# Dealing transposes out between short value products, and summing squares by transposes and row sums, in a hybrid decoder layer

## The chip, the cores and the metric

The kernel runs on one core of a Trainium2 chip. The metric is the device time of one execution in microseconds (us); lower is better. Three runs of the kernel before the change took 1103.09, 1104.46 and 1104.14 us. The chip's engines are named as in the profile: PE (TensorE matmuls), PEld (the weight loads of TensorE, which run beside its matmuls), DVE (VectorE), ACT (ScalarE), POOL (GpSimd) and SP (SyncE, which here issues the transfers).

## What is computed

One decoder layer on 1024 tokens of width 1024 in fp32, cut to what matters:

```python
h = rms_norm(x, ln_pre_mix)
proj = h @ w_in
q, k = rope(q, pos), rope(k, pos)
pool_out = multi_scale_pool(u_pool, w_pool, pool_scale)
attn_out = dilated_attention(q, k, v)
mix = concatenate([pool_out, attn_out]) @ w_out
x = x + rms_norm(mix, ln_post_mix)
h = rms_norm(x, ln_pre_ffn)
f = (silu(h @ w_gate) * (h @ w_up)) @ w_down
x = x + rms_norm(f, ln_post_ffn)

def rms_norm(x, g):
    return x * rsqrt(mean(x * x, axis=-1) + EPS) * g
```

The attention has 12 heads of dimension 64. Each head is evaluated under three (window, dilation) settings, (128, 1), (512, 4) and (2048, 16), and the three results are merged by their softmax denominators.

## The kernel before

**Numbers.** Activations lie with the channels on the 128 partitions and the tokens along the row. Every large product is made of fp32 numbers split in a high and a low part: hi is a copy rounded to the fast fp32 format, lo is the rest. A product is three matmuls (hi by hi, hi by lo, lo by hi), which is why most rows of the profile come in threes. A split is an ACT copy (hi) and a subtraction on DVE or POOL (lo): L340 and L344 for one family of weights, L1484 and L1486 for the gate and up weights, L1780 to L1782 for the down weights.

**Stages.** Norm and input projections; then attention; then the output projection, norm and residual (about 410 to 480 us), the SwiGLU block with its three large products (to about 1090), and the last norm with the residual. The 1024 tokens are worked in two halves of 512, and the heads in six pairs, so attention has 12 units (pair, half). Between the steps of a unit stand projection products as filling.

**Order.** The plan of the attention is a table of places (`put`, with a number per step) written by hand. All matmuls and transposes keep the order in which the program makes them: `mm` and `turned_to` both end in `keep_in_program_order`. DVE, ACT, POOL and SP take their order from a scheduler with priorities. PE reads its queue strictly in order.

**Values of a unit.** `values` makes the steps that turn probabilities into outputs. A step `turn` transposes three or four 128 x 128 tiles of the weighed probabilities `pp` on PE into a bank of PSUM (tag "t", of which there are two), by the matrix `pmt` or the identity `idt`; ACT then copies the bank to the hi part of `ptr` (L969) and DVE forms its lo part (L970). There are two buffers `ptr`. A step `product` multiplies the columns of `ptr` by the values `v`: per tile (or per two to four neighbouring tiles, if they share their keys) a pair of matmuls, one on the hi columns with 128 columns of weights, one on the lo columns with 64. Half 0 has three groups a head (4, 3 and 3 tiles), half 1 four groups of 4, of which two have four pairs of 128 columns each.

In six of the units (1, 3, 5, 7, 8 and 11, marked `tv`) turns and products are joined: the step `both(i)` makes the products of two groups, then the turns of the next two. In units 1, 3, 5, 7 and 11 that gives runs of 16 short products followed by 8 transposes. The other six units have turns and products as separate steps, each at its own place in the plan.

**Norms.** The sum of squares over the channels of a token crosses the partitions. For four of the norms (two halves of the norm after the mixer, two of the one ahead of the SwiGLU block) `Squares.add` collects the squares of eight blocks of channels in `sq` (ACT squares into `p`, DVE adds), and `Squares.mean` multiplies each 128 tokens of `sq` by a column of ones, which leaves 128 sums in the rows of a bank: four matmuls of one column, each in two passes, so eight records in the trace. `rsqrt_mean` takes them through ACT (L365, and L369 for a second use of the sum) and a power of -0.5 on POOL (L370). `Squares.rows` then spreads the result along the partitions with four transposes of `nrr`, and the norm's scaling on DVE reads them.

The last norm is in `End`. Its `mean` for half 0 multiplies both `sq` and the last block's squares `p`, which were not added yet, by the ones: twice four matmuls. Its first step behind the sums is on DVE (L367), then the power on POOL (L370).

Of the kernel before, what the change touches and what calls it, by code (L numbers as in the profile page):

```python
# [8 lines left out]
F32 = mybir.dt.float32  # L9
# [18 lines left out]
EARLY = 6  # L28

# [261 lines left out]
def hybrid_block(ctx: ExitStack, tc: tile.TileContext, xT, w_in, w_v, w_vp, w_pool, w_out, w_gate, w_up, w_down,  # L291
# [80 lines left out]


# [13 lines left out]
    ones = const.tile([P, 217], F32, name="ones")[:, :1]  # L387
# [556 lines left out]
    def values(pr, h):  # L944
# [7 lines left out]

        def turn(hd, gi):
            g = groups[gi]
            if h:
                need(("w", pr.p, h, hd, g[0][0]), 4)
            else:
                need(("w", pr.p, 0, hd), 4)
            await_(("t", 0), weighted(hd, gi))
            t = bank("t")  # L960
            for n, (kb, j) in enumerate(g if h == 0 else ()):
                turned_to(t[:, n * P:(n + 1) * P], un.row(hd, j)[:, kb * P:(kb + 1) * P], pmt)
            for n, (side, kb, qs, part) in enumerate(g if h else ()):
                turned_to(t[:, n * P:(n + 1) * P], un.pp[hd, side][:, qs, part * P:part * P + P],
                                    idt if side else pmt)
            w = len(g) * P
            ptr = turned[hd, gi] = att.tile([P, 2, 512], F32R, name="ptr", tag="ptr", bufs=PTB)
            with tc.high_priority(offset=rank("t", pr, h)):
                nc.scalar.activation(ptr[:, 0, :w], t[:, :w], AF.Copy)  # L969
                nc.vector.tensor_tensor(ptr[:, 1, :w], t[:, :w], ptr[:, 0, :w].bitcast(F32), ALU.subtract)  # L970
            turned_in(("ptr", pr.p, h, hd, gi))

        def product(hd, gi):
# [11 lines left out]
            if h == 0:  # L985
                for kb in sorted({kb for kb, j in g}):
# [5 lines left out]
                    mm(oo[0:64], v[:, 0], ptr[:, 1, n * P:n * P + wd], start=False, stop=(kb == 3), skip_group_check=True)  # L992
                    n += 4 - kb
            while h and n < len(g):
# [5 lines left out]
                else:  # L1000
# [7 lines left out]
                   start=False, stop=last, skip_group_check=True)  # L1008
                n += wd // P
# [15 lines left out]
        def both(i):  # L1025
            old, new = ids[max(0, 2 * i - 2):2 * i], ids[2 * i:2 * i + 2]
            if i:
                await_(*([("t", 0), ("t", 1)] if new else []),
                       *(weighted(*a) for a in new),
                       *(("ptr", pr.p, h, *a) for a in old), ("v", pr.p, h))  # L1030
            for a in old:
                product(*a)
            for a in new:
                turn(*a)
        return ([lambda a=a: turn(*a) for a in ids], [lambda a=a: product(*a) for a in ids],
# [162 lines left out]
    for u, (pr, h) in enumerate(units):  # L1198
# [12 lines left out]
        def part(n, i, a=(pr, h), box=box):  # L1211
# [849 lines left out]
```

## Time and profile before

| | us |
|---|---|
| runs of the kernel, three | 1103.09, 1104.46, 1104.14 (median 1104.14) |
| the profiled execution: span from the first to the last instruction | 1101.3 |
| what lies around the span, against the median | 2.8 |
| DMA, mean over the span | 183 GB/s |
| POOL, the power L370 of the norms, 128x4, five times | 1.10 each |
| DVE, row sum L871 (128x128 to 128x32), six times | 0.28 each |

The profiled execution's own time is its span and what lies around it; differences worked out in the span carry over to the time as they are.

How to read the rows. A row of the timeline is: start in us from the span's start, length in us, engine, line of the kernel, operation, result <- operands, for a matmul the size of the array used, shapes, how many such instructions in a row, and in brackets how long the engine idled ahead of it and what ended that. A run's length goes from its first start to its last end; the instructions in it overlap, since PE is pipelined. A row of groups has the count, then the busy time and the mean ns of one, then the idle time ahead of them with what ended it.

### The profile page before, as it was taken

Reading aid. Unit: us, or ns where it says so; the run is one execution under the profiler, and the core shown is the slowest. Engines: PE = TensorE matmul, PEld = TensorE weight load, DVE = VectorE, ACT = ScalarE, POOL = GpSimd, SP = SyncE. Lnnn points to the kernel's source line nnn. Section 1 sums busy time; section 2 is a strip of 40 time slices with the busy share of each in tenths; the row PEclk is TensorE's granted clock in tenths of the full one; section 3 lists DMA queues with packets and bytes.
Section 4 is the critical chain, followed back from the end, with each engine's and each line's share of the span. In section 5 each row is a group of like instructions: output and inputs, shape, how many; then the busy total and the mean of one; then the engine's idle time right before and its main releaser. Section 6 shows DMA issues by size and latency. Waiting matters only on the chain.

```text
span 1101.3 us, 16033 instructions
## 1 busy us (share of the span) xinstructions
PE 1091.4 (99%) x5653; PEld 930.7 (85%) x5653; DVE 796.7 (72%) x1350; ACT 553.8 (50%) x994; POOL 519.9 (47%) x421
## 2 busy tenths in 40 slices
PE   9999999999999999999999999999999999999998
PEld 7888999998898888888888888888888888888887
DVE  7967878777977758799677778576566576343674
ACT  7456767676777855765322222233222534343432
POOL 0001616263654120100677777677568958666521
PEclk9999999999999999999999999999999999999999
DMA  8225232424248448554466766443455878656442
GB/s 297 96 83 182 97 135 78 153 94 156 77 173 325 173 147 302 222 199 168 179 235 240 239 241 227 172 172 134 143 200 199 291 265 281 207 182 201 134 153 77
DMA packets 91296, 201.81 MB, mean 183 GB/s; under 512 B 9296, under 2 KB 25168, under 8 KB 89808
## 3 DMA queue, kind: packets, MB, share of 16 engines
q1 hardware_dynamic: 90240, 200.00, 51.8%
q8 instruction: 44, 0.72, 0.3%
q10 hardware_dynamic: 976, 0.79, 0.2%
q14 instruction: 36, 0.29, 0.1%
HBM read 143.87 MB, written 56.89 MB: 182 GB/s over the span
## 4 chain that ended last, share of the span: by engine, by line
PE 97%; ACT 1%; DVE 1%; DMA 0%; issue 0%; POOL 0%; ACTq 0%; DVEq 0%
PE ps_pj L296 31%; PE ps_s L296 26%; PE ps_o L296 26%; PE ps_t L296 10%; PE ps_t L299 3%; DMA wraw<-in_w_in_dram 0%; ACT pp L834 0%; PE ps_o L299 0%; ACT ptr L969 0%; ACT z L1302 0%; POOL rcl L538 0%; POOL rsw L535 0%; ACT whl L340 0%; DVE y L1899 0%; ACT k L557 0%
## 5 line engine op out<-in xcount | busy, mean ns | idle before, releaser
L296 PE MATMUL ps_o<-tT,fw 128*128 128x512 f32 x648 | 150.4, 389 | 0.0
L296 PEld LDWEIGHTS ps_o<-tT,fw 128*128 128x128 f32 x648 | 121.6, 188 | 25.2
L296 PE MATMUL ps_pj<-x,whl 128*128 128x512 f32 x480 | 130.6, 398 | 0.0
L1486 POOL TENSOR_TENSOR fw<-rw,fw 128x512 fp32r<-128x512 f32 x72 | 99.9, 1410 | 34.1 <-ACT fw L1484 34.1
L296 PEld LDWEIGHTS ps_pj<-x,whl 128*128 128x128 f32 x480 | 86.5, 188 | 14.0
L344 POOL TENSOR_TENSOR whl<-wraw,whl 128x512 fp32r<-128x512 f32 x42 | 57.4, 1389 | 49.7 <-ACT whl L340 41.0
L1781 POOL TENSOR_TENSOR op<-rw,op 128x512 fp32r<-128x512 f32 x38 | 61.2, 1611 | 39.4 <-ACT op L1780 38.5
L370 POOL TENSOR_TENSOR nrr<-nrr,half 128x4 f32<-128x4 f32 (+1 forms) x7 | 6.9, 984 | 141.2 <-ACT eps L369 99.0
L296 PE MATMUL ps_s<-b,fw 128*128 128x512 f32 x312 | 72.5, 389 | 0.0
L1782 DVE TENSOR_TENSOR op<-rw,op 128x512 fp32r<-128x512 f32 x33 | 46.0, 1394 | 34.3 <-ACT op L1780 32.2
L1780 ACT ACTIVATE op<-rw 128x1024 fp32r<-128x1024 f32 x38 | 40.1, 1058 | 59.4 <-PE ps_t L296 31.8
L296 PEld LDWEIGHTS ps_s<-b,fw 128*128 128x128 f32 x312 | 58.6, 188 | 12.2
L1486 POOL TENSOR_TENSOR whl<-rw,whl 128x512 fp32r<-128x512 f32 x30 | 47.8, 1615 | 40.8 <-ACT whl L1484 34.4
L1484 ACT ACTIVATE fw<-rw 128x1024 fp32r<-128x1024 f32 x45 | 47.5, 1062 | 38.6 <-PE ps_o L296 15.5
L296 PE MATMUL ps_pj<-whl,x 128*128 128x256 f32 (+1 forms) x432 | 64.3, 297 | 0.0
L970 DVE TENSOR_TENSOR ptr<-ps_t,ptr 128x512 fp32r<-128x512 f32 (+1 forms) x84 | 53.0, 647 | 12.8 <-ACT ptr L969 11.8
L969 ACT ACTIVATE ptr<-ps_t 128x512 fp32r<-128x512 f32 (+1 forms) x84 | 45.1, 561 | 29.1 <-PE ps_t L299 21.3
L296 PEld LDWEIGHTS ps_pj<-whl,x 128*128 128x128 f32 x432 | 57.3, 191 | 2.3
L834 ACT ACTIVATE pp<-pp,sx 128x256 f32<-128x256 f32 x96 | 47.8, 501 | 6.4 <-DVE sx L831 5.9
L1781 POOL TENSOR_TENSOR fw<-rw,fw 128x512 fp32r<-128x512 f32 x26 | 41.6, 1602 | 19.3 <-ACT fw L1780 18.7
L296 PE MATMUL ps_pj<-b,fw 128*128 128x512 f32 x216 | 50.3, 389 | 0.0
L296 PE MATMUL ps_o<-ptr,v 128*128 128x128 f32 (+3 forms) x376 | 49.8, 268 | 0.0
(336 smaller groups left out, 2771.5 us busy)
## 6 DMA issues: line engine op xcount, KB each, us to landing
rw<-bd SPq DMA_DIRECT2D x77, 256.0 KB, 4.2
rw<-in_w_gate_dram SPq DMA_DIRECT2D x28, 512.0 KB, 4.6
rw<-in_w_up_dram SPq DMA_DIRECT2D x28, 512.0 KB, 5.4
v<-vd SPq DMA_DIRECT2D x22, 512.0 KB, 4.9
rw<-wsd SPq DMA_DIRECT2D x44, 256.0 KB, 3.9
bd<-p SPq DMA_DIRECT2D x39, 256.0 KB, 2.1
rw<-in_w_down_dram SPq DMA_DIRECT2D x33, 256.0 KB, 4.3
wraw<-in_w_out_dram SPq DMA_DIRECT2D x15, 512.0 KB, 5.2
```

The source lines that it names most:

```text
L296: return tc.keep_in_program_order(nc.tensor.matmul(*a, **k))
L299: return tc.keep_in_program_order(nc.tensor.transpose(dst, src, by))
L344: pin(eng.tensor_tensor(dst[:, 1, at:at + w], src[:, at:at + w], dst[:, 0, at:at + w].bitcast(F32), ALU.subtract))
L370: powers.append(nc.gpsimd.tensor_tensor(r, r, half.to_broadcast([P, n]), ALU.pow))
L834: nc.scalar.activation(pt[:, j, lo:], pt[:, j, lo:], AF.Exp, bias=sx[:, 0, side, j, hd, 0:1], scale=-1.0, accum_out=sx[:, 0, side, j, hd, ...
L969: nc.scalar.activation(ptr[:, 0, :w], t[:, :w], AF.Copy)
L970: nc.vector.tensor_tensor(ptr[:, 1, :w], t[:, :w], ptr[:, 0, :w].bitcast(F32), ALU.subtract)
L1484: nc.scalar.activation(dst[:, :, 0], src, AF.Copy)
L1486: low[0] = eng.tensor_tensor(dst[:, i, 1], src[:, i], dst[:, i, 0].bitcast(F32), ALU.subtract)
L1780: nc.scalar.activation(w[:, :, 0], raw, AF.Copy)
L1781: nc.gpsimd.tensor_tensor(w[:, 0, 1], raw[:, 0], w[:, 0, 0].bitcast(F32), ALU.subtract)
L1782: (nc.gpsimd if p == "P1" else nc.vector).tensor_tensor(w[:, 1, 1], raw[:, 1], w[:, 1, 0].bitcast(F32), ALU.subtract)
```

## The change

Two things change.

**Turns in pieces.** A class `Turn` holds one group's transposes and can issue them one at a time (`one`) or all that are left (`rest`, which also makes the copies to `ptr`). `both` puts the next two groups into a list `guests` before it makes the products, and `product` calls `between` after each pair of matmuls: if the pair was 128 columns wide, one transpose of the next groups is issued there. In the units that turn and multiply apart, a product may host the next turn if its place in the plan lies less than NEAR behind the product; NEAR is 0.0, so none does.

**Sums of squares.** A function `column_sums` transposes each 128 tokens of the squares by `idt` into a bank and lets DVE add up each row (a reduction 128 x 512 to 128 x 4, into a tile `sums`). `Squares.mean` uses it in place of the products by ones for its four norms, and `End.mean` for half 0, where DVE first adds `p` to `sq`. Half 1 of the last norm and the first norm of the layer keep their ones. A tile of ones shrinks from 217 to 177 columns.

```diff
+NEAR = 0.0
...
+    def column_sums(srcs, n, tags):
+
+        name = "sums%d" % count[0]
+        count[0] += 1
+        sums = const.tile([P, n], F32, name=name, tag=name)
+        parts = [(src, c) for src in srcs for c in range(src.shape[-1] // P)]
+        for b in range(0, len(parts), 4):
+            t = bank(tags[b // 4 % len(tags)])
+            for i, (src, c) in enumerate(parts[b:b + 4]):
+                turned_to(t[:, i * P:(i + 1) * P], src[:, c * P:(c + 1) * P], idt)
+            w = len(parts[b:b + 4])
+            nc.vector.tensor_reduce(sums[:, b:b + w], t[:, :w * P].rearrange("p (c x) -> p c x", c=w), op=ALU.add,
+                                    axis=mybir.AxisListType.X)
+        return sums
...
+        class Turn:
+
+            def __init__(self, hd, gi):
+                self.at, self.g, self.n, self.t = (hd, gi), groups[gi], 0, None
+
+            def one(self):
+                hd, gi = self.at
+                if self.n == len(self.g):
+                    return False
+                if self.t is None:
+                    need(("w", pr.p, h, *((hd, self.g[0][0]) if h else (hd,))), 4)
+                    await_(("t", 0), weighted(hd, gi))
+                    self.t = bank("t")
+                to, job = self.t[:, self.n * P:(self.n + 1) * P], self.g[self.n]
...
+                self.n += 1
+                return True
+
+            def rest(self):
+                while self.one():
+                    pass
...
+        guests = []
+
         def turn(hd, gi):
...
+            if not (guests and guests[0].at == (hd, gi)):
+                guests.insert(0, Turn(hd, gi))
+            guests.pop(0).rest()
+
+        def between(wd):
+            if wd == P:
+                for g in guests:
+                    if g.one():
+                        return
...
                 mm(oo[0:64], v[:, 0], ptr[:, 1, n * P:n * P + wd],
                    start=False, stop=last, skip_group_check=True)
+                between(wd)
...
+            guests.extend(Turn(*a) for a in new)
             for a in old:
                 product(*a)
             for a in new:
                 turn(*a)
...
-            sp = self.sp if self.on_pe else bank(self.tag)
-            for c in range(0 if self.on_pe else n):
-                mm(sp[:, c:c + 1], self.sq[:, c * P:(c + 1) * P], ones, start=True, stop=True)
+            sp = self.sp if self.on_pe else column_sums([self.sq], n, (self.tag,))
             self.r = rsqrt_mean(sp[:, :n], n, "nr", None, self.to)
...
             def mean():
+                at = 4 * self.h + lo // P
+                if not self.h:
+                    sq = self.sq[:, lo:hi]
+                    nc.vector.tensor_tensor(sq, sq, self.jk[lo], ALU.add)
+                    box["r"] = rsqrt_mean(column_sums([sq], n, (tags[0],)), n, "nr", eps[:, at:at + n])
+                    return
                 busy(3)
```

What the change moves in the engines' queues, at three places. First PE in unit 1: the products of two groups by the values (`ps_o<-ptr,v`), the transposes of the next probabilities (`ps_t<-pmt,pp`) and the scores behind them (`ps_s<-k,qh`). Before:

```order
L296 MATMUL ps_o<-ptr,v_951 64x128
L296 MATMUL ps_o<-ptr,v_953 128x128
L296 MATMUL ps_o<-ptr,v_953 64x128
L296 MATMUL ps_o<-ptr,v_953 128x128
L296 MATMUL ps_o<-ptr,v_953 64x128
L296 MATMUL ps_o<-ptr,v_953 128x128
L296 MATMUL ps_o<-ptr,v_953 64x128
L296 MATMUL ps_o<-ptr,v_953 128x128
L296 MATMUL ps_o<-ptr,v_953 64x128
L299 MATMUL ps_t<-pmt,pp 128x128 x8
L296 MATMUL ps_s<-k,qh 128x256
```

The end of the same run in the changed kernel (rows with 128 in front of the x are hi, with 64 lo):

```order
L297 MATMUL ps_o<-ptr,v_953 128x128
L297 MATMUL ps_o<-ptr,v_953 64x128
L300 MATMUL ps_t<-pmt,pp 128x128
L297 MATMUL ps_o<-ptr,v_953 128x128
L297 MATMUL ps_o<-ptr,v_953 64x128
L300 MATMUL ps_t<-pmt,pp 128x128
L297 MATMUL ps_o<-ptr,v_953 128x128
L297 MATMUL ps_o<-ptr,v_953 64x128
L300 MATMUL ps_t<-pmt,pp 128x128
L297 MATMUL ps_s<-k,qh 128x256
```

Seven of the eight transposes have moved from behind the run to a place between two pairs; the eighth stands where it stood. Over the kernel 76 transposes have moved so.

Second, DVE around the norm after the mixer, half 1, at about 458 to 465 us: splits of gate and up weights (`fw<-rw`, `whl<-rw`), squares added up (`sq<-sq,p`) and the first step of the SwiGLU block (`p<-ps_pj,r`). Before:

```order
L1486 TENSOR_TENSOR fw<-rw,fw 128x512 x2
L1381 TENSOR_TENSOR sq<-sq,p 128x512 x2
L1486 TENSOR_TENSOR whl<-rw,whl 128x512 x2
L1486 TENSOR_TENSOR fw<-rw,fw 128x512 x4
L1507 TENSOR_TENSOR p<-ps_pj,r_4720 128x512
```

And now:

```order
L1539 TENSOR_TENSOR fw<-rw,fw 128x512 x2
L1436 TENSOR_TENSOR sq<-sq,p 128x512
L1539 TENSOR_TENSOR whl<-rw,whl 128x512 x2
L1436 TENSOR_TENSOR sq<-sq,p 128x512
L1539 TENSOR_TENSOR fw<-rw,fw 128x512 x4
L387 TENSOR_REDUCE sums_5171<-ps_o 128x4
L1560 TENSOR_TENSOR p<-ps_pj,r_4720 128x512
```

The reduction comes in between the four splits and the SwiGLU step; one of the additions of squares has changed places with a pair of splits.

Third, DVE at the sums of the last norm, half 0, at about 1030 to 1037 us, with splits of the down weights (`op`, `fw`, `whl`) around the additions of squares. Before:

```order
L1782 TENSOR_TENSOR whl<-rw,whl 128x512
L1809 TENSOR_TENSOR sq<-sq,p 128x512 x2
L1782 TENSOR_TENSOR op<-rw,op 128x512
L1782 TENSOR_TENSOR fw<-rw,fw 128x512
L1782 TENSOR_TENSOR op<-rw,op 128x512
L367 SCALAR_TENSOR_TENSOR nrr<-ps_t,eps 128x4
```

And now:

```order
L1835 TENSOR_TENSOR whl<-rw,whl 128x512
L1862 TENSOR_TENSOR sq<-sq,p 128x512 x2
L1835 TENSOR_TENSOR op<-rw,op 128x512
L1881 TENSOR_TENSOR sq<-sq,p 128x512
L1835 TENSOR_TENSOR fw<-rw,fw 128x512
L387 TENSOR_REDUCE sums_9393<-ps_t 128x4
L1835 TENSOR_TENSOR op<-rw,op 128x512
L368 SCALAR_TENSOR_TENSOR nrr<-sums_9393,eps 128x4
```

The new addition has come ahead of the split of `fw`, and the reduction behind it, ahead of a split of `op`.

More of the change, by code (lines that the diff above doesn't have):

```diff
@@ L371, in rsqrt_mean @@
         return r
+    count = [0]
+    def column_sums(srcs, n, tags):
[11 more added lines that the diff above has]
+        return sums
     right, left = ExitStack(), ExitStack()
@@ L386, in hybrid_block @@
             nc.gpsimd.memset(qlow[h][64 - 64 * a:128 - 64 * a, a].bitcast(F32), 0.0)
-    ones = const.tile([P, 217], F32, name="ones")[:, :1]
+    ones = const.tile([P, 177], F32, name="ones")[:, :1]
     nc.vector.memset(ones, 1.0)
@@ L951, in weighted @@
             return "w", pr.p, h, (8 * hd + 8 - 4 * groups[gi][0][0] if h else 4 * hd + 4)
-        def turn(hd, gi):
[L954 to L971, printed above, removed]
+        class Turn:
[10 more added lines that the diff above has]
+                to, job = self.t[:, self.n * P:(self.n + 1) * P], self.g[self.n]
+                if h:
+                    side, kb, qs, part = job
+                    turned_to(to, un.pp[hd, side][:, qs, part * P:part * P + P], idt if side else pmt)
+                else:
+                    kb, j = job
+                    turned_to(to, un.row(hd, j)[:, kb * P:(kb + 1) * P], pmt)
+                self.n += 1
[3 more added lines that the diff above has]
+                    pass
+                t, w = self.t, len(self.g) * P
+                ptr = turned[self.at] = att.tile([P, 2, 512], F32R, name="ptr", tag="ptr", bufs=PTB)
+                with tc.high_priority(offset=rank("t", pr, h)):
+                    nc.scalar.activation(ptr[:, 0, :w], t[:, :w], AF.Copy)
+                    nc.vector.tensor_tensor(ptr[:, 1, :w], t[:, :w], ptr[:, 0, :w].bitcast(F32), ALU.subtract)
+                turned_in(("ptr", pr.p, h, *self.at))
@@ L1008, in product @@
                    start=False, stop=last, skip_group_check=True)
+                between(wd)
                 n += wd // P
@@ L1034, in both, with hosted @@
                 turn(*a)
-        return ([lambda a=a: turn(*a) for a in ids], [lambda a=a: product(*a) for a in ids],
+        def hosted(a, b):
+            if b is not None:
+                guests.append(Turn(*ids[b]))
+            product(*ids[a])
+        return ([lambda a=a: turn(*a) for a in ids], [lambda b=None, i=i: hosted(i, b) for i in range(len(ids))],
                 [lambda i=i: both(i) for i in range(len(ids) // 2 + 1)])
@@ L1209, in hybrid_block, with part @@
         box = []
-        def part(n, i, a=(pr, h), box=box):
+        def part(n, i, *x, a=(pr, h), box=box):
             if not box:
                 box.append(values(*a))
-            box[0][n][i]()
+            box[0][n][i](*x)
         if G["tv"][u]:
@@ L1218, in hybrid_block @@
         else:
-            put([lambda i=i, f=part: f(0, i) for i in range(ng)], u + g["t0"], u + g["t1"])
-            put([lambda i=i, f=part: f(1, i) for i in range(ng)], u + g["v0"], u + g["v1"])
+            t, v = ([g[a + "0"] + (g[a + "1"] - g[a + "0"]) * i / ng for i in range(ng)] for a in "tv")
+            for i in range(ng):
+                near = [b for b in range(i + 1, ng) if 0 <= t[b] - v[i] < NEAR]
+                put([lambda f=part, i=i: f(0, i)], u + t[i], 0)
+                put([lambda f=part, i=i, b=near[0] if near else None: f(1, i, b)], u + v[i], 0)
     for p, at in enumerate(G["vt"]):
@@ L1833, in mean @@
                 busy(4)
-                at = 4 * self.h + lo // P
                 box["r"] = rsqrt_mean(sp[:, :n], n, "nr", eps[:, at:at + n])
```

## The prediction

> **What bounds the kernel now.** I read the busy shares first, then the chain that ended last, then the busy time by stretch.
>
> ```profile
> PE 1091.4 (99%) x5653; PEld 930.7 (85%) x5653; DVE 796.7 (72%) x1350; ACT 553.8 (50%) x994; POOL 519.9 (47%) x421
> PE 97%; ACT 1%; DVE 1%; DMA 0%; issue 0%; POOL 0%; ACTq 0%; DVEq 0%
> ```
>
> Behind the stretch and its length, the windows view gives the busy time of PE, of the weight loads (PEld), of DVE, ACT and POOL, then the granted clock and the share and rate of the DMA engines.
>
> ```profile
> 100.00:460.00 360.00, 358.97 (x2236) 320.37 (x2235) 286.81 (x693) 261.86 (x591) 135.11 (x145) 1.00 0.44 157
> 480.00:1090.00 610.00, 610.00 (x2790) 508.99 (x2789) 411.83 (x475) 219.09 (x266) 369.35 (x255) 1.00 0.56 196
> ```
>
> TensorE is the bound nearly everywhere: 97% of the chain, 358.97 of 360 us in the attention half, 610.00 of 610 in the feed-forward half, at a granted clock of 1.00. So a nanosecond taken off PE's in-order queue is a nanosecond off the end, as long as nothing then arrives late. A full queue is not an efficient one, though: PE counts as busy while a product waits for its weights to be loaded. That is what the first half of the change works on. All changes below are read as changes of PE's end-to-end pitch, the distance from the end of one instruction to the end of the next.
>
> **Part 1: transposes dealt out between short products.** The first value-product run of unit 1, as the timeline shows it (start, length, count):
>
> ```profile
> 118.96 1.49 PE L296 MATMUL ps_o<-ptr,v 128*128 128x128 f32 x16
> 120.28 1.06 PE L299 MATMUL ps_t<-pmt,pp 128*128 128x128 f32 x8
> 121.10 0.36 PE L296 MATMUL ps_s<-k,qh 128*128 128x256 f32 x1
> 121.30 0.28 PE L296 MATMUL ps_s<-k,ql 128*128 128x256 f32 x1
> ```
>
> the groups of such products and transposes over the whole span (count, then busy time and mean ns of one):
>
> ```profile
> L296 PE MATMUL ps_o<-ptr,v 128*128 128x128 f32 x122 | 23.1, 259 | 0.0
> L299 PE MATMUL ps_t<-pmt,pp 128*128 128x128 f32 x216 | 31.6, 274 | 0.1
> ```
>
> and a run of transposes between long products, elsewhere:
>
> ```profile
> 457.30 0.84 PE L296 MATMUL ps_pj<-b,whl 128*128 128x512 f32 x3
> 457.98 0.60 PE L299 MATMUL ps_o<-idt,nrr 128*128 128x128 f32 x4
> 458.34 0.94 PE L296 MATMUL ps_pj<-b,whl 128*128 128x512 f32 x3
> ```
>
> Four pitches come out of these rows.
> - A product whose weights are ready costs its streaming alone. The two 256-wide products end at 121.46 and 121.58, 0.12 apart, so a 128-wide one costs 0.06. This is hi to lo: the lo product has only 64 columns of weights to load.
> - Lo to hi: the 16 products take 1.49. A single one takes 0.259, so 15 pitches take 1.23. Eight are hi to lo, 0.48; the other seven are (1.23 - 0.48) / 7 = 0.107. So each hi product loses about 0.05 waiting for its 128 columns.
> - Transpose to transpose: the run of four takes 0.60 and a single one 0.274, so three pitches take 0.326, and one 0.109.
> - Lo to transpose: the products end at 120.45 and the eight transposes at 121.34, 0.89 later. Seven pitches of 0.109 are 0.763, which leaves 0.127: behind a short product the first transpose comes 0.018 later than behind another one.
>
> What the trace of before never shows is a transpose followed by a 128-wide product. The nearest row is the transpose followed by a 256-wide one: last transpose 121.34, next product 121.46, again 0.12, its streaming and nothing else. The full 128-column load for it was hidden behind the 0.109 of the transpose. So I take transpose to hi as 0.06, its floor; its ceiling is the 0.109 of transpose to transpose, should a transpose hide no more of a product's load than of its own kind's.
>
> Now the count. In the order of the changed kernel 76 transposes move from the run behind to a place behind a pair. Ten runs of 16 products (units 1, 3, 5, 7, 11, two each) take seven each, since the eighth stays behind the last pair; five shorter runs of the same units and one of unit 8 take one each. The units that turn and multiply in separate steps get none, because the limit for it, NEAR, is 0. Each moved transpose replaces (lo to hi 0.107 + one step of the transposes' run 0.109 = 0.216) by (lo to transpose 0.127 + transpose to hi 0.06 = 0.187): **0.029 less**. 76 x 0.029 = 2.2 us. With the ceiling it is 0.127 + 0.109 - 0.216 = 0.020 more, +1.5 us; if the 0.018 that the transpose comes late vanishes instead, 0.047 less, -3.6 us.
>
> The Trainium skill (page "TensorE: Matmul & The Clock Gate", "Back-to-back issue gap" and "LDWEIGHTS (loading the stationary operand)") has a rule that speaks against this part: a load takes the column count over 1.2, an estimate of 107 ns for 128, against N/2.4 + 2.5 = 56 ns of streaming, with the next load pulled ahead behind the running product. The trace agrees on lo to hi (0.107) and hi to lo (0.06). But by that rule a transpose, with 128 columns streamed, would hide only 56 ns of the load behind it, and a moved transpose would save nothing; this is the first rival below. The row at 121.10 speaks against it.
>
> Does a moved transpose wait for anything? It reads probabilities that were weighed before the product run began and were needed in the same step before; it writes a bank that is free, since the product that hosts it already reads the copy made from that bank. What it delays is the products between which it stands, by no more than the run's own length, and the copy of the transposed tiles still starts behind the eighth. That one ends a little earlier, not later. On DVE, ACT, POOL and SP only a handful of neighbours swap. I cost that at nothing; PE's idle time of 1.03 us in 360 is the cover.
>
> **Part 2: sums of squares by transposes and a row sum.** Five norms lose products against a column of ones, each recorded twice, and get four transposes, a reduction on DVE, and so one more step in the chain to the scaled rows. In order of time they are (1) and (3), after the mixer, halves 0 and 1, (2) and (4), ahead of the feed-forward block, and (5), the last, half 0. The last norm has both kinds:
>
> ```profile
> 1033.89 0.84 PE L296 MATMUL ps_t<-op 128*128 128x512 f32 x3
> 1034.57 0.95 PE L296 MATMUL ps_t<-ones,sq 128*128 128x1 f32 x8
> 1035.38 1.03 PE L296 MATMUL ps_t<-ones,p 128*128 128x1 f32 x8
> 1036.27 0.96 PE L296 MATMUL ps_pj<-fw 128*128 128x512 f32 x3
> ```
>
> ```profile
> 461.17 0.84 PE L296 MATMUL ps_pj<-b,whl 128*128 128x512 f32 x3
> 461.85 0.95 PE L296 MATMUL ps_o<-ones,sq 128*128 128x1 f32 x8
> 462.66 1.65 PE L296 MATMUL ps_pj<-b,whl 128*128 128x512 f32 x6
> L296 PE MATMUL ps_o<-tT,fw 128*128 128x512 f32 x648 | 150.4, 389 | 0.0
> ```
>
> A long product costs 150.4 / 648 = 0.232. From 462.01 to 464.31 stand eight ones records and six long products: 2.30 - 1.392 = 0.908 for the eight. From 458.14 to 459.28 stand four transposes and three long products: 1.14 - 0.696 = 0.444. So four transposes save **0.46** a norm. For the sixteen: 1034.73 to 1037.23 is 2.50 - 0.70 = 1.80, and 1.36 is saved, because a DVE add takes the place of the second set.
>
> What each saving leaves depends on the chain behind it. The reduction (128 x 512 from a bank to 128 x 4) is not in this trace. The nearest rows:
>
> ```profile
> L871 DVE TENSOR_REDUCE sx<-em 128x32 f32<-128x128 f32 x6 | 1.7, 280 | 0.1
> 464.42 0.69 DVE L1507 TENSOR_TENSOR p<-ps_pj,r 128x512 f32<-128x512 f32 x1 [3.46 <-PE ps_pj L296]
> ```
>
> By elements, four times the small reduction is 1.12 at most; an operation that reads 512 elements a partition from a bank takes 0.69. I take that, the row of the same size, with 0.28 and 1.12 as ends.
>
> The first norm (1), the second (2) and the fourth (4) have room. In each: what DVE does before the reduction, the power on POOL, and PE's load for the rows that wait for it.
>
> ```profile
> 414.52 1.22 DVE L344 TENSOR_TENSOR xk<-wraw,xk 128x1024 fp32r<-128x1024 f32 x1
> 416.50 1.02 POOL L370 TENSOR_TENSOR nrr<-nrr,half 128x4 f32<-128x4 f32 x1 [2.45 <-ACT nrr L365]
> 418.71 0.58 PEld L299 LDWEIGHTS ps_o<-idt,nrr 128*128 128x128 f32 x4
> 451.73 1.29 DVE L1486 TENSOR_TENSOR whl<-rw,whl 128x512 fp32r<-128x512 f32 x2 [0.41 <-ACT whl L1484]
> 455.05 0.18 ACT L365 ACTIVATE nrr<-ps_o 128x4 f32<-128x4 f32 x1
> 455.31 1.45 POOL L370 TENSOR_TENSOR nrr<-nrr,half 128x4 f32<-128x4 f32 x1 [37.79 <-ACT eps L369]
> 457.76 0.58 PEld L299 LDWEIGHTS ps_o<-idt,nrr 128*128 128x128 f32 x4
> 527.85 1.01 POOL L370 TENSOR_TENSOR nrr<-nrr,half 128x4 f32<-128x4 f32 x1 [61.25 <-ACT eps L369]
> 533.62 0.60 PE L299 MATMUL ps_pj<-idt,nrr 128*128 128x128 f32 x4
> ```
>
> (1) The power ends at 417.52 and is wanted at 418.71: 1.19 to spare. The transposes end 0.46 earlier than the ones did, the reduction puts 0.69 and a hand-over of some 0.05 in: 0.3 later, against PE 0.46 earlier, leaves 0.4. The reduction is queued behind the split of xk, which ends at 415.74, about when the transposes do. (2) The reduction stands behind the split of whl (to 453.02) and ends near 453.7; ACT reaches its step at 455.05 for other reasons, so nothing shifts, and of 457.76 - 456.76 = 1.0 half is left. (4) has 4.8. All three keep their saving: **-1.4 us**.
>
> Norm (3) does not have room:
>
> ```profile
> 462.83 0.17 ACT L365 ACTIVATE nrr<-ps_o 128x4 f32<-128x4 f32 x1 [1.55 <-PE ps_o L296]
> 463.08 1.01 POOL L370 TENSOR_TENSOR nrr<-nrr,half 128x4 f32<-128x4 f32 x1 [6.32 <-ACT nrr L365]
> 464.14 0.41 PEld L299 LDWEIGHTS ps_o<-idt,nrr 128*128 128x128 f32 x4 [0.27 <-POOL nrr L370]
> ```
>
> Here the load for the rows already waits for POOL (464.09). With the change the transposes end at 462.01 + 0.44 = 462.45; DVE is idle (the 3.46 us ahead of 464.42, above), so the reduction runs 462.48 to 463.17, ACT to 463.37, POOL 463.45 to 464.46, and the load starts at 464.51 instead of 464.14. PE, which would have been there 0.46 earlier, waits 0.83: **+0.37 us**. Nothing else of PE's may pass it; what stands behind, projections and the scaled rows, is late by that much. By the ends of the reduction it is -0.04 to +0.80.
>
> Norm (5) hangs on DVE:
>
> ```profile
> 1033.11 0.68 DVE L1782 TENSOR_TENSOR op<-rw,op 128x512 fp32r<-128x512 f32 x1
> 1033.71 1.77 DVE L1782 TENSOR_TENSOR fw<-rw,fw 128x512 fp32r<-128x512 f32 x1
> 1033.23 1.69 POOL L1781 TENSOR_TENSOR fw<-rw,fw 128x512 fp32r<-128x512 f32 x1 [0.60 <-DVE sq L1809]
> 1037.71 1.01 POOL L370 TENSOR_TENSOR nrr<-nrr,half 128x4 f32<-128x4 f32 x1
> 1040.95 0.58 PEld L299 LDWEIGHTS ps_o<-idt,nrr 128*128 128x128 f32 x4
> ```
>
> The new add of sq and p takes the place in DVE's queue at 1033.71, ahead of the split of fw. That slot lies beside POOL's split (1033.23 to 1034.92), and an operation of this size took 1.77 there against 0.68 without it. So the add ends near 1035.48, and the four transposes, which PE reaches at about 1034.5, end near 1036.1 in place of 1036.41, the end of the ones. Of the 1.36 about 1.0 is waited: **-0.36 us**, between 0 (the add still later by 0.4) and -1.36 (the add done in time). Behind it DVE's fw, reduction and op come 0.9 later; the power has 2.2 us to spare (1038.72 against 1040.95). The Trainium skill (page "SBUF — State Buffer", "Who interferes with whom") gives the cause: DVE's operation on two SBUF inputs and GpSimd's reads share a port, while a reduction on this chip never contends. The 1.77 agrees.
>
> **The sum**: -2.2 - 1.4 + 0.37 - 0.36 = -3.6 us. The profiled execution has a span of 1101.3; some 2.8 lie around it up to the median of 1104.14, and both stay. 1104.1 - 3.6 = **1100.5 us**.
>
> **Rivals.**
> - *A transpose hides no load* (0.109 from transpose to hi): +1.5 from part 1, -1.4 from part 2, no difference: 1104.2. For it: transposes follow each other at 0.109, like products short of weights. Against it: the 256-wide product behind the transposes paid nothing. Chance 0.12.
> - *A transpose hides everything and is not late itself*: -3.6 from part 1, -1.4 from part 2: 1104.1 - 5.0 = 1099.1. Against it is the 0.127, which the same rows show. Chance 0.10.
> - *The reductions turn room into waits*: DVE takes its queue in order, and if the split of xk stays tied to its transfer while PE is 2.2 us ahead, the reduction of norm (1) still ends near 416.4 and the power at 417.7, where PE, at 418.71 - 2.2 - 0.46 = 416.05, wants it: 1.7 lost there, and at (2) a wait like that of norm (3), 0.8: 1100.5 + 2.5 = 1103.0. For it: ACT's room there is small. Against it: the products' results set off those splits, so they shift with PE. Chance 0.14, a third of it still faster.
> - *Slower*: the weight load behind a transpose starts only when the transpose ends. Then transpose to hi is the load, bounded by all of lo to hi, 0.107, plus the streaming, 0.06; each insert costs 0.127 + 0.167 - 0.216 = 0.078 more, in all +5.9: 1104.1 + 5.9 - 1.4 = 1108.6. It decides from 0.107 on, where 76 x 0.018 uses up part 2's gain. The 0.12 at 121.46 speaks against it, though it is from a wider product. Chance 0.07.
> - The change doing nothing would need the inserts not to be there; the order has all 76.
>
> **How the numbers follow.** The forecast has 0.57 and its own range of 1099 to 1101.9; with the second rival 0.67, and 0.05 of the third, lie below the median by more than 0.2%, about what a measurement of this kernel can tell from no change (2.2 us). So faster 0.72; same 0.21 (first rival 0.12, rest of the third 0.09); slower 0.07. The range 1097.6 to 1104.2 takes in the first three rivals and the ends of the reductions' cost, and leaves out the slower one.
>
> **What would show it.** In the changed profile a run of products and transposes of unit 1 should take about 7 x 0.029 = 0.20 less from 118.96's counterpart to the scores behind it; a load of hi behind a transpose that shows as a step of more than 0.06 would break part 1. The load for norm (3)'s rows should show a wait on POOL of some 0.8, the transposes of norm (5) one on DVE of some 1.0, and norms (1), (2), (4) none. If PE's busy time does not fall by about 5.4 us (2.2 + 4 x 0.46 + 1.36), the prices are wrong; if it does and the span does not follow, the waits are.

## The result, and the profile after

| | before | after | ratio, 95% interval |
|---|---|---|---|
| median of ten runs, us | 1104.27 | 1101.88 | 0.9980 (0.9972 to 0.9988) |
| span of the profiled execution, us | 1101.3 | 1100.4 | |

The changed kernel is 2.4 us faster, 0.2%. The two spans differ by only 0.9 us, and the reason for that stands at the very start, as the next tables show. In every execution whose span is on record, 1.7 to 1.9 us lie around the span (1102.19 beside 1100.4 for the profiled one of the changed kernel). The 2.8 of the kernel before is thus some 1.8 and another 1.0 by which its profiled execution was quicker than the median; the forecast is not touched by it, since it goes from the median. The page of the changed kernel, with the lines that answer to those of before:

```profile
PE 1089.1 (99%) x5625; PEld 926.3 (84%) x5625; DVE 784.7 (71%) x1356; ACT 555.1 (50%) x994; POOL 524.4 (48%) x421
PE 89%; DVE 4%; ACT 2%; issue 2%; DMA 1%; POOL 1%; SPq 0%; ACTq 0%; DVEq 0%; POOLq 0%
```

PE has 28 instructions fewer (48 records by ones replaced by 20 transposes) and is 2.3 us less busy. The second line, the chain that ended last, shows what is new: PE's share fell from 97% to 89%, since the chain now leaves PE at waits that were not there and follows other engines back from them. The share doesn't say what those waits cost; that is read from the differences below.

To see where time came and went, the two traces were laid beside each other instruction by instruction: for each matmul that both kernels have, the end in the one less the end in the other, set to zero at 118.9 us, just ahead of the first value products of unit 1. Below, the same reckoning for all profiled executions, in us against the first profile of the kernel before (negative is earlier). The first column is the time in that profile; the row "start" is what had been lost by 118.9.

```
                 before   after  after  insert  sums   n3_    u1_    n5_    three_
                 again           again  _only   _only  early  later  late   moved
start             0.33    1.10   0.15   1.17   -0.24   0.07   0.69   0.21   0.27
133.5 (2 runs)    0.00   -0.43  -0.43  -0.43    0.00  -0.43  -0.43  -0.43  -0.43
150  (wait ptr)   0.00    0.09   0.04   0.04    0.04  -0.06  -0.62   0.00  -0.62
191  (unit 3)     0.00   -0.22  -0.33  -0.31    0.07  -0.39  -0.93  -0.34  -0.97
414  (attention)  0.01   -1.08  -1.15  -1.31    0.15  -1.35  -1.81  -0.95  -2.12
463.5 (norms 1-3) 0.01   -2.43  -2.50  -1.31   -1.20  -2.69  -3.08  -2.30  -3.46
465  (rows of 3)  0.01   -1.55  -1.62  -1.30   -0.33  -2.50  -2.20  -1.42  -3.28
530  (norm 4)     0.01   -2.02  -2.08  -1.31   -0.79  -2.96  -2.66  -1.89  -3.73
700  (blocks)     0.75   -1.71  -0.66  -1.10    0.68  -1.69  -1.70  -1.87  -3.71
1042 (norm 5)     0.75   -2.04  -0.99  -1.10    0.35  -2.03  -2.03  -2.87  -4.74
```

Two columns are the same kernel as another, so rows in which they differ are no work of the change: the start (-0.24 to 1.17 here, and 2.02 in one more) and the first blocks of the feed-forward part, 530 to 700 us. The rest repeats within 0.2 us up to unit 3 and at the norms; between unit 3 and 414 us it differs by up to 0.4. Part 1 of the change is read at 414: 0.95 to 1.35 us earlier in the five profiles that have the attention of the changed kernel (after, after again, insert_only, n3_early, n5_late). Part 2 is the sum of the norms' steps: in the first profile after, -0.94 from 414 to 530 and -0.33 at the last norm, 1.27 together. That makes some 2.4 of the forecast 3.6, and it is what the medians show.

The first product run of unit 1 in the changed kernel, from PE's timeline:

```profile
120.06 0.28 PE L297 MATMUL ps_o<-ptr,v 128*128 128x128 f32 x2
120.18 0.29 PE L300 MATMUL ps_t<-pmt,pp 128*128 128x128 f32 x1
120.23 0.37 PE L297 MATMUL ps_o<-ptr,v 128*128 128x128 f32 x2
120.43 0.30 PE L300 MATMUL ps_t<-pmt,pp 128*128 128x128 f32 x1
...
121.96 0.29 PE L300 MATMUL ps_t<-pmt,pp 128*128 128x128 f32 x1
122.01 0.36 PE L297 MATMUL ps_s<-k,qh 128*128 128x256 f32 x1
```

The eight transposes start 0.254 apart (120.18 to 121.96, seven steps), each with a pair ahead of it. Forecast was 0.127 + 0.06 + 0.06 = 0.247. And the scores behind the run stand 0.193 earlier than before: 0.028 an insert, against a forecast of 0.029.

What follows two runs later in unit 1. First the kernel before, DVE's low parts for the queries (`ql`) and for `ptr`, and the third group of value products on PE:

```profile
133.97 1.40 DVE L565 TENSOR_TENSOR ql<-rco,qh 64x512 fp32r<-64x512 f32 x2
135.41 1.29 DVE L970 TENSOR_TENSOR ptr<-ps_t,ptr 128x512 fp32r<-128x512 f32 x2
136.03 1.17 PE L296 MATMUL ps_o<-ptr,v 128*128 128x256 f32 x8
```

Then the same in the changed kernel, where the first lo product and its load (PEld) show a wait:

```profile
135.15 1.40 DVE L583 TENSOR_TENSOR ql<-rco,qh 64x512 fp32r<-64x512 f32 x2
136.58 1.29 DVE L1001 TENSOR_TENSOR ptr<-ps_t,ptr 128x512 fp32r<-128x512 f32 x2
136.71 0.28 PE L297 MATMUL ps_o<-ptr,v 128*128 128x256 f32 x1
137.33 1.05 PE L297 MATMUL ps_o<-ptr,v 128*64 128x256 f32 x7 [0.34 <-DVE ptr L1001]
137.33 1.02 PEld L297 LDWEIGHTS ps_o<-ptr,v 128*64 128x64 f32 x8 [0.55 <-DVE ptr L1001]
```

DVE's two rows stand 1.17 later, which is the 1.10 of the start and nothing of the 0.43 that PE had gained. The transposes themselves were done long before (the last started at 133.70); the low part of `ptr` stands behind `ql` in DVE's queue. That queue was nearly full: in the kernel before DVE had only two waits in the 19 us up to 136.7, 0.98 for POOL's part of the rotary work (`rsw`) and 0.35 for ACT's `pp`. And it did not come earlier with PE: with each profile's start taken off, the second of the two low parts ends between 136.64 and 136.77 in all twelve profiles, whatever PE does. So PE arrives earlier and waits: all 0.43 us are given back, and a little more.

Norm 3, all engines, with the new reduction:

```profile
460.99 0.60 PE L300 MATMUL ps_o<-idt,sq 128*128 128x128 f32 x4
461.62 0.69 DVE L387 TENSOR_REDUCE sums<-ps_o 128x4 f32<-128x512 f32 x1 [0.91 <-PE ps_o L300]
462.35 0.20 ACT L366 ACTIVATE nrr<-sums 128x4 f32<-128x4 f32 x1 [1.93 <-DVE sums L387]
462.63 1.01 POOL L371 TENSOR_TENSOR nrr<-nrr,half 128x4 f32<-128x4 f32 x1 [6.15 <-ACT nrr L366]
463.69 0.41 PEld L300 LDWEIGHTS ps_o<-idt,nrr 128*128 128x128 f32 x4 [1.15 <-POOL nrr L371]
463.70 0.65 PE L300 MATMUL ps_o<-idt,nrr 128*128 128x128 f32 x4 [0.72 <-POOL nrr L371]
```

The reduction took the 0.69 us that it was put at, and the chain behind it is as forecast, hand-over by hand-over: the load for the rows now idles 1.15 us, of which 0.27 was there before. The saving of 0.46 is followed by a loss of 0.88.

Norm 5, from the add of the squares to the reduction:

```profile
1032.90 1.42 POOL L1834 TENSOR_TENSOR fw<-rw,fw 128x512 fp32r<-128x512 f32 x1 [0.88 <-ACT fw L1833]
1033.10 1.77 DVE L1881 TENSOR_TENSOR sq<-sq,p 128x512 f32<-128x512 f32 x1
1034.92 0.42 PEld L300 LDWEIGHTS ps_t<-idt,sq 128*128 128x128 f32 x4 [1.22 <-DVE sq L1881]
1035.61 0.69 DVE L387 TENSOR_REDUCE sums<-ps_t 128x4 f32<-128x512 f32 x1
1036.22 0.96 DVE L1835 TENSOR_TENSOR op<-rw,op 128x512 fp32r<-128x512 f32 x1
```

The add beside POOL's split took 1.77 us, the duration that stood in that slot before, and PE's load waits 1.22 for it.

### The profile page after: what moved, and what is told of

Its sections match the earlier page's. It is cut to its first block, busy times and chain, and to the rows that moved or that the text cites. A ratio compares the mean times of both kernels' runs of the same rounds, so it can differ in the third digit from the quotient of the medians.

```text
span 1100.4 us, 15984 instructions
## 1 busy us (share of the span) xinstructions
PE 1089.1 (99%) x5625; PEld 926.3 (84%) x5625; DVE 784.7 (71%) x1356; ACT 555.1 (50%) x994; POOL 524.4 (48%) x421
## 4 chain that ended last, share of the span: by engine, by line
PE 89%; DVE 4%; ACT 2%; issue 2%; DMA 1%; POOL 1%; SPq 0%; ACTq 0%; DVEq 0%; POOLq 0%
PE ps_pj L297 27%; PE ps_o L297 25%; PE ps_s L297 24%; PE ps_t L297 10%; PE ps_t L300 3%; DMA rw<-in_w_gate_dram 1%; DVE z L1467 0%; DMA wraw<-in_w_in_dram 0%; DVE ptr L1001 0%; DVE z L1468 0%; ACT pp L852 0%; ACT ptr L1000 0%; PE ps_o L300 0%; ACT p L1435 0%; POOL nrr L371 0%
## 5 line engine op out<-in xcount | busy, mean ns | idle before, releaser
L1835 DVE TENSOR_TENSOR op<-rw,op 128x512 fp32r<-128x512 f32 x33 | 29.2, 885 | 39.9 <-ACT op L1833 33.8
L297 PE MATMUL ps_o<-ptr,v 128*128 128x128 f32 (+3 forms) x376 | 55.8, 274 | 0.4 <-DVE ptr L1001 0.3
L297 PEld LDWEIGHTS ps_o<-ptr,v 128*128 128x128 f32 x376 | 47.9, 167 | 4.6 <-DVE ptr L1001 1.4
```

Of the source, the lines that this page charges most:

```text
L297: return tc.keep_in_program_order(nc.tensor.matmul(*a, **k))
L1835: (nc.gpsimd if p == "P1" else nc.vector).tensor_tensor(w[:, 1, 1], raw[:, 1], w[:, 1, 0].bitcast(F32), ALU.subtract)
```

## The experiments

All are edits of the changed kernel, except for the two repeats.

**Each half alone.** In the first, the norms sum by ones again (both places of the change in `Squares.mean` and `End.mean` taken back); in the second, no transpose is dealt out:

```diff
-            if wd == P:
+            if False:
                 for g in guests:
```

> The transposes are dealt out as in the changed kernel; all five norms keep their products by ones. Theory A (the inserts save what was forecast on TensorE, some 0.19 us in each of ten runs and 0.03 in six single places, 2.1 in all, but unit 1 gives its share back in a wait for the low part of ptr, and smaller waits take another 0.4): from the first product run of unit 1 to the end of attention TensorE's rows come 1.0 to 1.3 us earlier than in the kernel before, and nothing is gained or lost behind; time 1.0 to 1.3 us under the kernel before. Rival B (what is missing was lost to the sums and the start, not to waits in attention): 1.9 to 2.2 us earlier at the end of attention.

> The five norms sum by transposes and row sums as in the changed kernel; every transpose of probabilities stays behind its run of products. Theory A (the norms' gains and waits do not depend on the inserts): norms 1, 2 and 4 save 0.46 us each, norm 3 costs 0.4, norm 5 saves 0.33; together 1.3 us under the kernel before, and no wait in unit 1 for the low part of ptr beyond that of the kernel before. Rival B (the reductions use the room that the inserts make): norm 3 or 5 differs from the changed kernel by more than 0.2 us.

The inserts alone: 1.31 us earlier at the end of attention, time 1103.37 us against 1104.06, ratio 0.9989 (0.9980 to 0.9998). Each of the ten runs does save, 0.15 to 0.19 us by the matched ends, 1.8 together; the six single places were to add some 0.2. The wait in unit 1 took 0.47 of it, and smaller waits the rest. Two of them show. At 255 us 0.11 is lost at a projection product, and between 0 and 0.36 in the other profiles with this attention. At 302 us the load of a lo product again waited for `ptr` in three of the five profiles, by 0.16 to 0.19, and not in the kernel before. So the loss lies in attention and belongs to the inserts, and rival B falls. The sums alone: -0.46 at each of norms 1, 2 and 4, a net loss of 0.41 at norm 3, -0.33 at norm 5, the same as with the inserts to 0.02 us; 1103.30 us, ratio 0.9991 (0.9982 to 0.9999). In unit 1 this kernel waits 0.05 more than the kernel before. By these ratios the halves are worth 1.2 and 1.0 us, with intervals from some 0.1 to 2; the medians, 0.7 and 0.8 apart, lie below what was expected. The two halves are independent at the norms to those 0.02 us, and their ratios multiply to 0.998.

**Norm 3's sums earlier.** The place of the sums in the plan:

```diff
- 'c1': (0.0979, 0.11685, 0.19849, 0.31663, 0.2738, 0.5795, 1.07088, 1.31702, 0.49893, 0.67018),
+ 'c1': (0.0853, 0.11685, 0.19849, 0.31663, 0.2738, 0.5795, 1.07088, 1.31702, 0.49893, 0.67018),
```

> The changed kernel with the sums of norm 3 (after the mixer, half 1) placed four long products, 0.9 us, earlier in TensorE's order; the scaled rows stay where they are. Theory A (the wait for the power is the reduction's own length in a chain without room): the wait of 1.15 us on the load for the rows falls to 0.3 or less, and TensorE is 0.8 to 0.9 us earlier behind it than in the changed kernel. Rival B (the reduction is held by the four splits ahead of it in VectorE's queue, which end near 460.7): it starts no earlier than before by more than 0.4 us, and half of the wait stays.

The edit moved three products, not four, so 0.70 us were to be had. DVE and the load for the rows:

```profile
459.64 0.69 DVE L387 TENSOR_REDUCE sums<-ps_o 128x4 f32<-128x512 f32 x1 [0.24 <-PE ps_o L300]
461.71 0.41 PEld L300 LDWEIGHTS ps_o<-idt,nrr 128*128 128x128 f32 x4 [0.46 <-POOL nrr L371]
```

The wait fell by 0.69 and PE's loss from 0.88 to 0.19: the chain's length was the cause. That is 0.46 where 0.3 or less was expected, for want of the fourth product. DVE was still free 0.24 us ahead of the reduction, so its queue did not hold it. One execution, 1101.16 us; its blocks of the feed-forward part took back 1.3 us of what it had won (table, 530 to 700).

**Unit 1's last joint step later.**

```diff
         1: {'t1': -0.0014,
...
-            'v1': -0.1282,
+            'v1': -0.1082,
```

> The changed kernel with the last joint step of unit 1 placed later in the plan: six projection products of 256 columns, 0.7 us of work, come ahead of the third group of value products in place of behind it. Theory A (the low part of ptr is late because VectorE's queue there goes by the rotary work and not by TensorE, so that TensorE gave back what it had gained): the wait of 0.55 us for ptr in that place falls under 0.1, and at 150 us TensorE stands 0.4 to 0.5 us earlier against the first run of unit 1 than in the changed kernel, and keeps that to the end of unit 3. Rival B (unit 1 as a whole is held by VectorE, ScalarE or GpSimd): the wait turns up at a later place of unit 1 or 2, and at 176 us the gain is under 0.15 us.

DVE's `ptr` and the products that read it:

```profile
136.09 1.29 DVE L1001 TENSOR_TENSOR ptr<-ps_t,ptr 128x512 fp32r<-128x512 f32 x2
137.01 1.15 PE L297 MATMUL ps_o<-ptr,v 128*128 128x256 f32 x10
```

There is no wait left. With the start's 0.69 taken off, `ptr` ends at 136.69 as in the kernel before (136.70): DVE did not move, PE came later, with other work ahead of it. At 191 us PE stands 0.6 to 0.7 us earlier than in the two executions of the changed kernel, and at 414 still 0.7. That is more than the 0.43 given back, because 0.19 of a wait that the kernel before had in the same place went as well. Rival B, that the unit as a whole is held by other engines, falls. The one execution took 1101.79 us; its feed-forward blocks took back 1.0.

**Norm 5's transposes later, and two repeats.**

```diff
- 'e0': ((0.26, 0), (0.42, 0), (0.47, 0.9)),
+ 'e0': ((0.295, 0), (0.42, 0), (0.47, 0.9)),
```

Beside this edit, both kernels were profiled once more, to see what differs from execution to execution. The three expectations, the two repeats first:

> The kernel before once more, to see which of the differences between two profiles are no work of the change. Theory A (the start and the feed-forward block differ from execution to execution): TensorE's rows differ from the first profile of the same kernel by several tenths of a microsecond up to 60 us, by under 0.1 from there to the end of attention, and by up to 0.3 in all in the first six blocks of the feed-forward part (540 to 680 us). Rival B (what was seen there belongs to the change): under 0.1 us at all three places.

> The changed kernel once more. Theory A (the wait for ptr in unit 1 and the net cost of norm 3 belong to the change, the waits in the blocks of the feed-forward part hang on when transfers land): unit 1's wait costs 0.35 to 0.55 us and norm 3 nets a loss of 0.4 again, while the waits between 540 and 680 us differ from the 0.3 us of the first profile by 0.2 or more. Rival B: all within 0.1 us of the first profile.

> The changed kernel with the transposes for the last norm's sums (half 0) three long products, 0.7 us, later in TensorE's order. Theory A (TensorE only waits there for VectorE's add of the squares, which stands beside GpSimd's split): the wait of 1.2 us on the load of the first transpose falls to 0.5 or less, the norm's net gain grows from 0.33 to about 1.0 us, and the rows behind are not waited for. Rival B (the add moves later with TensorE's order, or the rows become late): the net gain stays under 0.5 us.

DVE's add and the load that waits for it, with the transposes later:

```profile
1032.04 1.77 DVE L1881 TENSOR_TENSOR sq<-sq,p 128x512 f32<-128x512 f32 x1
1033.87 0.42 PEld L300 LDWEIGHTS ps_t<-idt,sq 128*128 128x128 f32 x4 [0.54 <-DVE sq L1881]
```

The add takes as long as ever, but PE has three products to do meanwhile: the load's wait falls from 1.22 to 0.54, the net gain of norm 5 is 1.0 us in place of 0.33, and nothing behind it waits; the one execution took 1100.46 us. The two repeats (1104.20 us before, 1102.30 after) show what is not the change's. Both kernels stumble in the blocks of the feed-forward part, in some executions and not in others, at the same matmul. The kernel before, second profile, and then the changed kernel, second profile:

```profile
594.08 0.69 DVE L1669 TENSOR_TENSOR sq<-ps_o,q 128x512 f32<-128x512 f32 x1 [2.62 <-DMA bd<-sq]
594.92 1.83 PE L296 MATMUL ps_o<-tT,fw 128*128 128x512 f32 x7 [0.49 <-DVE sq L1669]
```

```profile
592.48 0.69 DVE L1722 TENSOR_TENSOR sq<-ps_o,q 128x512 f32<-128x512 f32 x1 [3.25 <-DMA bd<-sq]
593.32 1.85 PE L297 MATMUL ps_o<-tT,fw 128*128 128x512 f32 x7 [1.14 <-DVE sq L1722]
```

DVE may not overwrite `sq` until its write to memory has landed, and PE may not reuse the bank until DVE has read it. PE lost 0.73 us there in the one, 1.38 in the other, and nothing at this matmul in the first profiles of both. Theory A holds on these points, but for the size in the kernel before, where up to 0.3 was expected and 0.74 came; unit 1's wait (0.47 from 136 to 137) and norm 3's net loss (0.42) came again in the second profile of the changed kernel.

**The three moves together**, and then two things more: norm 3's sums three products earlier still, and NEAR at 0.1, which puts 13 transposes more behind pairs, one in unit 4 and the others late in attention, most of them in unit 10.

> The changed kernel with the three places moved together: unit 1's last joint step later, norm 3's sums earlier, norm 5's transposes later. Theory A (independent terms, each as it was seen or is expected by itself: 0.6, 0.7 and 0.7 us): 2.0 us less than the changed kernel up to the waits in the feed-forward blocks, of which 0.3 to 0.9 us may be taken back there; time 1.1 to 2.0 us under the changed kernel, 1099.9 to 1100.8 against 1104.1 of the kernel before. Rival B (the feed-forward blocks are held by the transfers, so that what is gained ahead of them is lost there): only norm 5's 0.7 us shows, 1101.2.

> The kernel with the three places moved, with two things more: the sums of norm 3 stand three long products earlier still, and with NEAR at 0.1 two of the units that turn and multiply apart take 13 transposes behind pairs. Theory A (each term by itself): the last 0.2 us of norm 3's wait goes, unless the reduction is held behind the splits in VectorE's queue, and the 13 inserts save 0.027 each, 0.35 us; TensorE stands 0.4 to 0.55 us earlier at 530 us than with the three moves alone; time 1099.0 to 1099.6. Rival B (the units take their gain back in waits for probabilities or ptr): under 0.2 us at 530.

The three together: 1099.81 us against 1103.76 on the same chip, ratio 0.9965 (0.9953 to 0.9978), the fastest kernel here; by the two ratios that is 1.7 us under the changed kernel, by the medians 2.1. In its profile, which is the quickest of its six executions (1098.73), PE is 3.73 earlier at 530 and 4.74 at 1042, with nothing lost between 530 and 700. The time is a little under the expected range, and rival B falls: the terms add up to at least their sum.

The wider one came to 1101.30 us, ratio 0.9974 (0.9965 to 0.9983), where 1099.0 to 1099.6 was expected. The two intervals overlap, but its profile shows rival B's mechanism: PE is 2.22 us earlier at 530 in place of 3.73. Against the three moves alone, a first 0.3 is lost behind the insert in unit 4, at about 215 us, and the largest piece, 1.0, at one place in unit 11:

```profile
390.24 1.28 DVE L1001 TENSOR_TENSOR ptr<-ps_t,ptr 128x512 fp32r<-128x512 f32 x2
390.98 0.27 PE L297 MATMUL ps_o<-ptr,v 128*64 128x128 f32 x1 [0.89 <-DVE ptr L1001]
```

Again a lo product waits for the low part of `ptr` in DVE's queue. This is one profile; that the new inserts alone brought this wait about was not tried apart. Norm 3's last loss did go: from 460 to 465 us it now gains 0.49, and 0.25 with the three moves alone.

**Transposes inside the pairs.** What does an insert save? Here it stands between hi and lo, the eighth of a run inside the last pair too:

```diff
+                between(wd)
                 mm(oo[0:64], v[:, 0], ptr[:, 1, n * P:n * P + wd],
                    start=False, stop=last, skip_group_check=True)
-                between(wd)
```

> The changed kernel with each dealt-out transpose inside its pair, between the hi and the lo product, in place of behind the pair. Theory A (the saving comes from the 128-column weight load of the next hi product, which a transpose ahead of it hides and a lo product doesn't): nothing is hidden now, since hi still follows lo; per insert hi to transpose 0.13, transpose to lo 0.06, lo to hi 0.11 against 0.28 for the same three without it, so a run of 16 products and 8 transposes of unit 1 takes about 0.2 us more than in the kernel before, in place of 0.19 less, and at the end of attention TensorE is 1.5 to 2.5 us later than in the kernel before; time 2.5 to 3.5 us over the changed kernel. Rival B (any mixing of transposes with short products saves, by keeping the queue from bunching weight loads of one kind): the run takes at least 0.1 us less than in the kernel before.

PE's timeline for the same run of unit 1:

```profile
120.23 0.28 PE L300 MATMUL ps_t<-pmt,pp 128*128 128x128 f32 x1
120.26 0.42 PE L297 MATMUL ps_o<-ptr,v 128*64 128x128 f32 x2
120.51 0.30 PE L300 MATMUL ps_t<-pmt,pp 128*128 128x128 f32 x1
...
122.34 0.30 PE L300 MATMUL ps_t<-pmt,pp 128*128 128x128 f32 x1
```

The steps are now 0.301 (120.23 to 122.34, seven) where 0.254 stood, and the run takes 0.197 more than before the change, as theory A put it. Rival B falls: mixing by itself saves nothing. By the ends of the single matmuls, hi comes 0.06 behind a transpose and 0.11 behind a lo product. So the saving is what hi loses to its 128-column load, and a transpose directly ahead of it hides that load.

The time, 1109.19 us, ratio 1.0046 (1.0032 to 1.0060), is 7.3 us over the changed kernel where 2.5 to 3.5 was expected, and some 4 us above what the pitches give (1104 + 2.2 - 1.3). The profile, of the slowest of the four executions (1110.22), shows 3.8 beyond the pitches in one place. In unit 7 PE stood for more than 2 us at the first transpose of a run, until DVE had come past a cast of 2.9 us to the low part of `ptr`. (The profile names DVE's `wd`, which ran right behind that low part and ended at 302.05, just as PE went on.)

```profile
298.33 2.91 DVE L582 CAST qh<-rco 64x512 fp32r<-64x512 f32 x2 [0.46 <-POOL rco L556]
301.27 0.69 DVE L1001 TENSOR_TENSOR ptr<-ps_t,ptr 128x512 fp32r<-128x512 f32 x1
302.11 0.30 PE L300 MATMUL ps_t<-pmt,pp 128*128 128x128 f32 x1 [2.14 <-DVE wd L792]
```

Behind that wait the granted clock fell, as the windows show (stretch and length; busy PE, PEld, DVE, ACT, POOL; clock; DMA share; GB/s):

```profile
300.00:303.50 3.50, 1.39 (x14) 1.42 (x15) 3.44 (x6) 2.05 (x5) 2.31 (x3) 1.00 0.40 121
303.50:310.00 6.50, 6.50 (x35) 5.78 (x34) 4.98 (x8) 2.19 (x4) 1.34 (x2) 0.74 0.30 99
```

PE was busy for 1.39 of 3.5 us, and the mean clock of the next 6.5 was 0.74; taken finer, it was 0.50 from 303.6 to 307.0 us and 1.00 again behind that. Up to 286 us the kernel had lost 1.2 us, by the pitches. Whether the other three executions had the same stop is not shown.

## Why the prediction was right, and which step failed

The time, 1101.88, lay in the range and on the side that was forecast, at the upper edge of the forecast's own 1099 to 1101.9; the change measured 2.4 us where 3.6 stood.

- **The bound**: right. PE's order sets the end, and what was saved on PE and not waited away came through.
- **The pitches of part 1**: right. 0.028 an insert against 0.029; the pitch from a transpose to hi, which no row of before showed, was its floor. The first rival, that a transpose hides no load, falls by the 0.254 of the rows; by the same rows the estimate from the Trainium skill (page "TensorE: Matmul & The Clock Gate", "Back-to-back issue gap" and "LDWEIGHTS (loading the stationary operand)"), a load of 107 ns behind a streaming of 56, does not hold where a transpose stands ahead of a product.
- **"I cost that at nothing; PE's idle time of 1.03 us in 360 is the cover"**: this step failed. Part 1 was put at 2.2 us and gave 0.95 to 1.35; the runs themselves saved 1.8, and waits took the difference. That PE hardly idled said that nothing was late as yet, not how much earlier PE could come before something was. In unit 1 the answer was in the trace before: the two low parts of `ptr` ended at 136.10 and 136.70, and the loads of the first lo products that read them started at 136.15 and 136.75, right behind. PE had no room there at all. The question that was asked (does the transpose wait for anything?) was the wrong one; the one to ask was which producer behind the run does not go by PE.
- **Norms 1, 2 and 4**: right, -0.46 each to 0.01 us, and no wait.
- **Norm 3**: right in mechanism and size, +0.42 against +0.37.
- **Norm 5**: right, -0.33 against -0.36, with the add at 1.77 as it was put. The reduction ran beside POOL's split of `op` without being slowed (0.69, as at norm 3, while the split of DVE behind it took 0.96), which is what the Trainium skill (page "SBUF — State Buffer", "Who interferes with whom") states of reductions.
- **PE's busy time**, as a check: a fall of 5.4 was asked for and 2.3 seen. The check was badly chosen: the start alone took 1.1 us more in this execution, with slower matmuls in it, and part of a wait is counted as busy (the 0.88 lost at norm 3 show as 0.72 of idle PE in its row). The matched ends show what the busy share can't.
- **The third rival** (room turning into waits) was the nearest to what happened, but it was placed at norms 1 and 2, which had room, and not in attention.

## What to carry to other kernels

In these runs of short products a transpose directly ahead of the widest weight load hides it; where it stands in the pair decides, 0.2 us a run one way or the other. Before a saving on the bounding engine is counted, look for the next instructions on it whose inputs come from a queue that does not go by that engine, and read how much room they have: a busy share of 99% says nothing of that. Where a saving brings a longer chain, move the producer up or the consumer down by as much as the chain grew; three such moves made 0.2% into 0.35% here.

## What the runs showed that was not expected

- The start of the kernel differs from execution to execution by up to 2.3 us by 118.9 us (-0.24 to 2.02 in eleven profiles but for the one of reference), nearly all of it in the first 10 us. In the first profile after, long matmuls there came some 0.43 apart up to 9.9 us, where 0.23 stood in the first profile before from 5 us on. Where the windows view shows a granted clock of 0.50, such matmuls come 0.43 apart too: from 303.6 to 307.0 us with the transposes inside the pairs, and from 8.17 to 11.59 us in the wider kernel, which lost most at its start (2.02). In the other profiles the view shows 1.00 at the start, so that the clock is the cause there too is likely and not shown. One span against another is no measure of a change of 2 us; ten runs of each are.
- Between 540 and 680 us, an execution loses 0 to 1.5 us, in the kernel before as in the changed ones, mostly at one matmul of each block, which waits by way of DVE for the write of `sq` to memory. How far PE is ahead does not set it: the kernel with the most lead (3.7 us) lost 0.0, the one with 0.8 lost 1.5.
- Some 2.1 us of PE idling in one stretch was followed by a granted clock of 0.50 for 3.4 us, 0.74 over the next 6.5 (the kernel with transposes inside the pairs, one profile).
